# Pinning the token forms of the second FFN just ahead of their products, and spreading the gate steps of the mixer

## The chip, the cores and the metric

One core of a Trainium2 chip runs the whole layer in one launch. The metric is the device time of one execution in microseconds (us), the median of three runs. Besides them there is one profiled execution, from which every row of a trace below is taken. The engines are TensorE (PE in the rows, its weight loads PEld), VectorE (DVE), ScalarE (ACT), GpSimd (POOL) and SyncE (SP); the last two only issue DMAs in the stretches that matter here.

## The reference, cut to what matters

The reference is one layer of a diffusion backbone on 256 latent tokens (with 256 context tokens beside them) of width 2048: a SwiGLU FFN, a mixer (attention heads and bidirectional mLSTM heads), a second SwiGLU FFN on the latents, and a final norm. The change touches the gates of the mLSTM heads and the up-projection of the second FFN:

```python
def half_step_ffn(x, mod, i, g, w_up, w_down):
    h = adaln(x, g, mod, i)
    a, b = jnp.split(h @ w_up, 2, axis=-1)
    return x + 0.5 * mod[:, i + 2, None, :] * ((jax.nn.silu(a) * b) @ w_down)
...
    aq, ak, av, mqk, mv, mo, gt = jnp.split(h @ w_in, SPLIT_POINTS, axis=-1)
...
    lf_f = jax.nn.log_sigmoid(gt[:, :, 1])
...
    b = jnp.cumsum(lf, axis=-1)
...
    m = jnp.maximum(inter, jnp.max(d_log, axis=-1))
```

Everything is in float32.

## The kernel before

**Weights in two parts.** Each float32 weight tile of 128 x 2048 is split in two halves of 128 x 1024. For each half ScalarE writes a rounded part `hi` (L124) and VectorE the rest, `lo = raw - hi` (L125). The tokens are kept in two such parts as well, and a product is three matmuls: hi by hi, lo by hi, hi by lo (L166, issued at L170). There are four `hi` and four `lo` buffers, so the split of a half can start when the product of the half four places earlier has been done.

**Who sets the order.** The instructions are written in a "trace order", and a scheduler then lays out one stream for each engine, which the engine runs strictly in that order. It takes, of the instructions that it believes to be ready, the one that stands earliest in the trace order; so an instruction whose operands are there early can move ahead of many that were traced before it. `pin(x)` ties `x` behind the instruction that was traced just before it on the same engine, and behind no other. `tc.issue_after(y)` ties an instruction behind `y` alone.

**The mixer's projection and the gates.** `project` runs a token-still projection in four groups of weights, each in four "parts" of 12 matmuls; `w_b` is the one here: 16 parts, numbered 0 to 15, of 384 columns. `gates` (L1333) is a generator of six steps that computes the mLSTM gates beside that projection:

1. `lf` (log-sigmoid of the forget gates, ScalarE and VectorE);
2. prefix sums by three small TensorE products (L1343, L1344), `bs`, `bt`, `u` on VectorE;
3. transposes of `u` and `bt` for direction 0 (L1355, L1359), copies `uT`, `btT`;
4. the same for direction 1;
5. a chain of small dependent VectorE operations on 8 partitions: `um` (L1364), `hc`, two maximum scans for each direction (L1382, L1385), `negM` with its DMA to DRAM on SP (L1390), and `hcd` (L1393);
6. a TensorE product with `hcd` (L1398), four small transposes (L1407), `hcb`, `wg`, `enm` and their exponentials.

`weave(..., 2)` puts them behind parts 1, 3, 5, 7, 9 and 11. Beside every part there also runs a step of `Beside` (L290 to L358): about once a part a VectorE product of 128 x 1024 with one half of a row of `w_mod` (L231, tiles `sr` and `early`), which is pinned, and one part later the DMA that refills the tile (L313, on SP, pinned too). After `w_b` come the `w_mk` projections.

**The second FFN.** Its weights come in eleven blocks of 512 hidden columns. Blocks 0 and 1 are computed by plain products; `up(1)` gives block 1 in eight "units" u0 to u7, each of one weight tile and 24 matmuls of 512 columns. From block 2 on, `quad(n)` computes a block by seven products, m0 to m6, of half the depth with combined tokens and combined weights (sums of weight tiles, made on the way by DMAs that add into `chain2c` and `chain2r`, and by a VectorE addition at L2207 that shows as L2150). Each product has two steps (q = 0, 1), each with one weight tile and 12 matmuls. The tokens are quarters a11, a12, a21, a22 of the normalised input; four combined "token forms" are made once by `token_forms` (L2078): `n1` = a22 - a21, `s2` = -n1 - a11, `s4` = -s2 - a12, and `s3` = a11 - a21, which overwrites a21. A form takes three (n1, s3) or two (s2, s4) VectorE operations on 128 x 1024 in a part of `acc2`, then a ScalarE copy (L2086) and one more VectorE subtraction. The order of the seven products is a11, a12, n1, s4, s2, s3, a22, and they are interleaved with units: two after m0, one after each of m1 to m6.

The start of this stage (L2328 to L2345) runs units u0, u1, u2, and after each of them asks for one form: n1, s2, s4. Then the first quad begins, and `s3` is asked for at step 7, that is after m3 and the unit behind it. The first operation of a difference is tied behind `gated` (L1993), the last VectorE operation of block 0's hidden values; the others are tied to nothing. The weights are asked for on SP (L2056): five at first, then one at each unit; `first_tiles` loads the first quad's tiles on SP (L2069), pinned: `chain2c` after unit u1's request, `chain2r` at step 1.

Of the kernel before, what the change touches and what calls it, by code (L numbers as in the profile page):

```python
# [54 lines left out]
def tile_layer(ctx: ExitStack, tc: tile.TileContext, I: dict, out: bass.AP):  # L55
# [13 lines left out]
    def bank():  # L69
        return ps["mm"].tile([P, 512], F32, tag="mm", name="mm")  # L70
# [66 lines left out]
    def load_split(src, n=2048):  # L137
        raw = raw_tile(n)
        nc.sync.dma_start(raw, src)
        wt = split(raw, n)  # L140
        next(beside["load"], None)
        return wt
# [80 lines left out]
    def conditions(cB, h0, h1, seqs=(CTX, LAT)):  # L223

        for s in seqs:
            nc.sync.dma_start(cB[s], ccd[s, h0 * 1024 : h1 * 1024].partition_broadcast(P))
# [63 lines left out]
    class Beside:  # L290
# [49 lines left out]
        def steps(self):  # L340
            half = None
            while self.n < len(self.items) or self.due or self.late:
                while self.n < len(self.items):
                    h = self.items[self.n][2]
                    if h != half:
                        half = h
                        conditions({LAT: self.cB}, h, h + 1, (LAT,))
                        self.waits += WAIT
                    if self.n not in self.slots or self.done < np.interp(self.n, *zip((0, 0), *self.pace)) + self.waits:
                        break  # L350
                    self.one()
                yield
                self.done += 1
                for x in [x for x in self.due if x[0] <= self.done]:
                    self.due.remove(x)
                    self.finish(*x[1:])
                if self.late and self.late[0][0] <= self.done:
                    mod_rows_out(*self.late.pop(0)[1:])  # L358

    def pin(ins):  # L360
        tc.keep_in_program_order(ins)
# [14 lines left out]
    def mod_rows_out(i, s, v):  # L376

        pg = tbank()
        tc.keep_in_program_order(nc.tensor.transpose(pg[:KT, :P], v, ident))
        gr = sm.tile([KT, P], F32, tag="gr", name="gr")  # L380
        nc.vector.tensor_copy(gr, pg[:KT, :P])
        nc.sync.dma_start(mod_rows[i][s, :].rearrange("(k p) -> k p", p=P), gr)
# [37 lines left out]
    def drain(it):  # L420
        for _ in it:
            pass

    def weave(main, side, every=1, skip=0):

        for n, _ in enumerate(main):
            if n >= skip and (n - skip) % every == every - 1:
                next(side, None)
# [302 lines left out]
    def pinned(ins):  # L731
        tc.keep_in_program_order(ins)
# [22 lines left out]
    with pool(name="f1u", bufs=1) as f1u:  # L755
# [44 lines left out]
        def token_forms():  # L800
            sub = lambda o, x, y: nc.vector.tensor_tensor(o, x, y, op=ALU.subtract)
            neg_sub = lambda o, x, y: nc.vector.scalar_tensor_tensor(o, x, -1.0, y, op0=ALU.mult, op1=ALU.subtract)

            def parts(s, x):
                return x[0][:, s].bitcast(F32), x[1][:, s].bitcast(F32)

            def put(dst, s, v):
                nc.scalar.activation(dst[0][:, s], v, AF.Copy)
                sub(dst[1][:, s], v, dst[0][:, s].bitcast(F32))

            vs = {}
            for s in range(2):
                v = vs[s] = sraw().rearrange("p (k c) -> p k c", k=8)
                (h1, l1), (h2, l2) = parts(s, a22), parts(s, a21)
                sub(v, h1, h2)
                nc.vector.tensor_tensor(v, v, l1, op=ALU.add)
                sub(v, v, l2)
                put(n1, s, v)
                yield
            for s in range(2):  # L820
                v = vs[s]
                h, l = parts(s, a11)
                neg_sub(v, v, h)
                sub(v, v, l)
                put(s2, s, v)
                yield
                h, l = parts(s, a12)
                neg_sub(v, v, h)
                sub(v, v, l)
                put(s4, s, v)  # L830
                yield
            for s in range(2):
                v = sraw().rearrange("p (k c) -> p k c", k=8)
                (h1, l1), (h2, l2) = parts(s, a11), parts(s, a21)
                sub(v, h1, h2)
                nc.vector.tensor_tensor(v, v, l1, op=ALU.add)
                sub(v, v, l2)
                put(s3, s, v)
                yield

        forms = token_forms()
# [176 lines left out]
    sub = lambda o, x, y: pinned(nc.vector.tensor_tensor(o, x, y, op=ALU.subtract))  # L1018
    neg_sub = lambda o, x, y: pinned(nc.vector.scalar_tensor_tensor(o, x, -1.0, y, op0=ALU.mult, op1=ALU.subtract))
# [229 lines left out]
    def products_of(bs, wt, n, ks, toks):  # L1249

        ps = []
        for j, k in enumerate(ks):
            for t in toks:
                tt = slice(t * P, (t + 1) * P)
                ps.append((bs[t], hhi[:, k, tt], hlo[:, k, tt], *wt(slice(j * n, (j + 1) * n)), k == 0, k == KT - 1))
        for ms in in_parts(products_in_order(ps), len(ks)):
            issue(ms)
            next(beside["part"], None)
            yield

    def project(name, n, toks, bs):

        bs.update({t: bank()[:, :n] for t in toks})
        for g in range(4):
            wt = load_split(I[name][g], 4 * n)
            yield from products_of(bs, wt, n, range(4 * g, 4 * g + 4), toks)
# [11 lines left out]
    with ExitStack() as mx:  # L1278
# [135 lines left out]

        gate_steps = gates()
        b_b = {}
        weave(project("w_b", 384, range(4), b_b), gate_steps, 2)
        ev_mv(3, 0, b_b)
        drain(gate_steps)

# [533 lines left out]
    with f2x:  # L1954
# [28 lines left out]
        for f in range(NPRE, FB):  # L1983
# [9 lines left out]
            gated = nc.vector.tensor_tensor(sa, sa, pab[1], op=ALU.mult)  # L1993
# [19 lines left out]
        QUADS = range(2, LAST + 1)  # L2013
# [53 lines left out]
        def first_tiles(ab, c, tiles):  # L2067
            for q in range(2):
                pin(nc.sync.dma_start(tiles[q], part(QUADS[0], ab, c + q)))  # L2069
# [8 lines left out]
        def token_forms():  # L2078

            sub = lambda o, x, y: nc.vector.tensor_tensor(o, x, y, op=ALU.subtract)  # L2080
            neg_sub = lambda o, x, y: nc.vector.scalar_tensor_tensor(o, x, -1.0, y, op0=ALU.mult, op1=ALU.subtract)
            f32 = lambda x: [y.bitcast(F32) for y in x]
            vs = [acc2[:, x, 1024:].rearrange("p (k c) -> p k c", k=8) for x in range(2)]

            def put(dst, v):
                nc.scalar.activation(dst[0], v, AF.Copy)  # L2086
                sub(dst[1], v, dst[0].bitcast(F32))

            def difference(v, x, y):
                (h1, l1), (h2, l2) = f32(x), f32(y)  # L2090
                with tc.issue_after(gated.ins):
                    sub(v, h1, h2)
                nc.vector.tensor_tensor(v, v, l1, op=ALU.add)
                sub(v, v, l2)

            def negative_less(v, x):
                h, l = f32(x)
                neg_sub(v, v, h)
                sub(v, v, l)

            v = vs[0]
            difference(v, a22, a21)
            put(n1, v)
            yield
            negative_less(v, a11)
            put(s2, v)
            yield
            negative_less(v, a12)
            put(s4, v)
            yield  # L2110
            v = vs[1]
            difference(v, a11, a21)
            put(s3, v)
            yield
# [204 lines left out]
        forms = token_forms()  # L2319
        plain_units = units()  # L2320

        def unit(n=1):
            for _ in range(n):
                next(plain_units)
                clock[0] += 2
                turned()

        ask(nc.sync, N_RAW)  # L2328
        for n in range(3):
            unit()  # L2330
            if n == 1:
                first_tiles(0, 0, sets[0])
            steps(forms)
        for n in QUADS:
            for step, _ in enumerate(quad(n)):
                clock[0] += 1
                turned()
                if n == QUADS[0] and step == 1:
                    first_tiles(1, 2, sets[1])
                if step % 2:  # L2340
                    late_one = step // 2 >= (5 if n == QUADS[0] else 4)
                    asking[0] = None if late_one else nc.gpsimd
                    unit(behind[n].get(step // 2, 0))
                if n == QUADS[0] and step == 7:
                    drain(forms)  # L2345
        before_final()
# [159 lines left out]
```

## Time and profile before

| | before |
|---|---|
| median of 3 runs | 2600.71 us (2599.49 to 2600.97) |
| the profiled execution's own time | 2603.62 us |
| its span, first to last instruction | 2601.9 us |
| mean granted TensorE clock | 0.994 |
| TensorE busy | 2572.8 us, 99% of the span |
| VectorE busy | 2176.1 us, 84% |
| ScalarE busy | 1440.0 us, 55% |
| DMA, mean rate | 263 GB/s |

A row of the timeline gives the start in us from the span's first instruction, the time it takes, the engine and the line of the kernel, the operation, the tile written and those read, shapes, how many instructions the row joins, and in brackets the idle time of the engine before it with what ended it. A row of the table by stretches gives for each engine its busy time and the number of instructions, then the granted TensorE clock (1.00 is full), the share of the DMA engines and the rate.

### The profile page before, as it was taken

Reading aid. Unit: us, or ns where it says so; the run is one execution under the profiler, and the core shown is the slowest. Engines: PE = TensorE matmul, PEld = TensorE weight load, DVE = VectorE, ACT = ScalarE, POOL = GpSimd, SP = SyncE. Lnnn points to the kernel's source line nnn. Section 1 sums busy time; section 2 is a strip of 40 time slices with the busy share of each in tenths; the row PEclk is TensorE's granted clock in tenths of the full one; section 3 lists DMA queues with packets and bytes.
Section 4 is the critical chain, followed back from the end, with each engine's and each line's share of the span. In section 5 each row is a group of like instructions: output and inputs, shape, how many; then the busy total and the mean of one; then the engine's idle time right before and its main releaser. Section 6 shows DMA issues by size and latency. Waiting matters only on the chain. (4 is left out here: it accounts for less than half of the span.)

```text
span 2601.9 us, 33899 instructions
## 1 busy us (share of the span) xinstructions
PE 2572.8 (99%) x12646; PEld 2144.4 (82%) x12646; DVE 2176.1 (84%) x2842; ACT 1440.0 (55%) x1876; POOL 263.6 (10%) x359
## 2 busy tenths in 40 slices
PE   8999999999999999999999999999999999999998
PEld 5788888888888888888889889888897888888886
DVE  7788888878888788888887788798888888888888
ACT  5454444444444465444454358467485766766664
POOL 0000000100000100010110000110001111111111
PEclk8999999999999999999999999999999999999999
DMA  9989999999999989889987887677757899999986
GB/s 391 354 216 267 270 284 275 258 275 285 261 286 271 274 245 241 221 212 229 226 248 252 291 299 242 233 265 258 263 217 272 262 277 273 270 274 271 278 255 188
DMA packets 127653, 684.70 MB, mean 263 GB/s; under 512 B 14200, under 2 KB 16760, under 8 KB 64896
## 3 DMA queue, kind: packets, MB, share of 16 engines
q0 software_dynamic: 42048, 284.18, 46.2%
q1 hardware_dynamic: 85440, 398.35, 41.3%
q8 instruction: 99, 1.62, 0.2%
q14 instruction: 66, 0.54, 0.1%
HBM read 664.59 MB, written 17.89 MB: 262 GB/s over the span
## 5 line engine op out<-in xcount | busy, mean ns | idle before, releaser
L124 ACT ACTIVATE hi<-raw 128x1024 fp32r<-128x1024 f32 (+2 forms) x488 | 498.3, 1038 | 356.0 <-PE mm L170 219.3
L125 DVE TENSOR_TENSOR lo<-raw,hi 128x1024 fp32r<-128x1024 f32 (+2 forms) x476 | 563.4, 1203 | 149.1 <-ACT hi L124 105.4
L170 PE MATMUL mm<-hi,hhi 128*128 128x512 f32 (+3 forms) x1024 | 392.7, 386 | 0.0
L170 PE MATMUL mm<-hi,hlo 128*128 128x512 f32 (+3 forms) x1024 | 386.3, 380 | 0.0
L124 ACT ACTIVATE hi<-chain 128x1024 fp32r<-128x1024 f32 x240 | 247.4, 1055 | 218.7 <-PE mm L170 110.0
L125 DVE TENSOR_TENSOR lo<-chain,hi 128x1024 fp32r<-128x1024 f32 x240 | 287.7, 1220 | 84.1 <-ACT hi L124 76.3
L170 PE MATMUL mm<-lo,hhi 128*128 128x512 f32 (+3 forms) x1024 | 253.3, 378 | 0.0
L231 DVE SCALAR_TENSOR_TENSOR junk<-sraw,cBh 128x1024 fp8e5<-128x1024 f32 x192 | 234.2, 1220 | 15.5 <-DMA sraw<-in_w_mt 13.2
L170 PEld LDWEIGHTS mm<-hi,hhi 128*128 128x128 f32 x1024 | 193.9, 189 | 31.5
L170 PEld LDWEIGHTS mm<-hi,hlo 128*128 128x128 f32 x1024 | 194.0, 189 | 31.0
L170 PEld LDWEIGHTS mm<-lo,hhi 128*128 128x128 f32 x1024 | 187.0, 188 | 33.1
L125 DVE TENSOR_TENSOR lo<-chain2c,hi 128x1024 fp32r<-128x1024 f32 x112 | 135.8, 1222 | 30.6 <-ACT hi L124 26.1
L124 ACT ACTIVATE hi<-chain2c 128x1024 fp32r<-128x1024 f32 x112 | 118.6, 1061 | 64.9 <-PE mm L170 46.9
L125 DVE TENSOR_TENSOR lo<-chain2r,hi 128x1024 fp32r<-128x1024 f32 x104 | 126.2, 1222 | 31.1 <-ACT hi L124 26.9
L124 ACT ACTIVATE hi<-chain2r 128x1024 fp32r<-128x1024 f32 x104 | 110.4, 1061 | 62.3 <-PE mm L170 45.5
L170 PE MATMUL mm<-lo,hid2h 128*128 128x512 f32 x352 | 136.9, 389 | 0.0
L170 PE MATMUL mm<-hi,hid2l 128*128 128x512 f32 x352 | 136.8, 389 | 0.0
L170 PE MATMUL mm<-hi,hid2h 128*128 128x512 f32 x352 | 135.8, 389 | 0.0
L754 POOL DMA_DIRECT2D chain<-in_w_up1b x60 | 52.7, 879 | 729.7 <-DVE lo L125 702.0
L231 DVE SCALAR_TENSOR_TENSOR sr<-sr,cBl 128x1024 f32<-128x1024 f32 x85 | 102.6, 1216 | 18.8 <-DMA sr<-in_w_mt 18.7
L170 PE MATMUL mm<-hhi,hi 128*128 128x512 f32 (+1 forms) x256 | 83.7, 346 | 0.0
L170 PE MATMUL mm<-hlo,hi 128*128 128x512 f32 (+1 forms) x256 | 81.1, 336 | 0.0
(518 smaller groups left out, 5759.2 us busy)
## 6 DMA issues: line engine op xcount, KB each, us to landing
chain<-in_w_up1b POOLq DMA_DIRECT2D x60, 1024.0 KB, 10.3
sraw<-in_w_mt SPq DMA_DIRECT2D x96, 512.0 KB, 7.8
raw<-in_w_dn POOLq DMA_DIRECT2D x48, 1024.0 KB, 12.5
chain2c<-in_w_up2b POOLq DMA_DIRECT2D x44, 1024.0 KB, 10.2
chain2r<-in_w_up2b POOLq DMA_DIRECT2D x42, 1024.0 KB, 10.2
sr<-in_w_mt SPq DMA_DIRECT2D x82, 512.0 KB, 5.6
raw<-in_w_up1b SPq DMA_DIRECT2D x40, 1024.0 KB, 7.9
mraw<-in_w_m SPq DMA_DIRECT2D x32, 1024.0 KB, 8.0
```

Of the source, the lines that this page charges most:

```text
L124: scalar[0].activation(hi, src, AF.Copy)
L125: vector[0].tensor_tensor(lo, src, hi.bitcast(F32), op=ALU.subtract)
L170: tensor[0].matmul(o, st_, mv, start=first, stop=last, skip_group_check=skip)
L231: ins = nc.vector.scalar_tensor_tensor(junk() if junk else raw, raw, 1.0, cB[s], op0=ALU.mult, op1=ALU.mult, accum_out=mT[:, i, s, kt, h : ...
L754: accum = lambda dst, src: nc.gpsimd.dma_start(dst, src, accum_op=ALU.add)
```

## The change

In the mixer the six gate steps no longer stand behind every second part: five stand behind parts 1, 3, 5, 10 and 14, and the sixth is drained after the projection and after `ev_mv`, ScalarE's copies of the projection's results. In the second FFN the form n1 is asked for after unit u1 (before: after u0), s2 after step 1 of the first quad, s4 after step 3, and s3 after step 7 as before; the first VectorE operation of each form is pinned.

```diff
@@ mixer: the gates beside the projection w_b
-        weave(project("w_b", 384, range(4), b_b), gate_steps, 2)
+        for n, _ in enumerate(project("w_b", 384, range(4), b_b)):
+            if n in (1, 3, 5, 10, 14):
+                steps(gate_steps)
         ev_mv(3, 0, b_b)
         drain(gate_steps)
@@ second FFN: token_forms
             def difference(v, x, y):
                 (h1, l1), (h2, l2) = f32(x), f32(y)
-                with tc.issue_after(gated.ins):
-                    sub(v, h1, h2)
+                pin(sub(v, h1, h2))
                 nc.vector.tensor_tensor(v, v, l1, op=ALU.add)
                 sub(v, v, l2)
 
             def negative_less(v, x):
                 h, l = f32(x)
-                neg_sub(v, v, h)
+                pin(neg_sub(v, v, h))
                 sub(v, v, l)
@@ second FFN: where the forms are asked for
             if n == 1:
                 first_tiles(0, 0, sets[0])
-            steps(forms)
+                steps(forms)
@@ in the first quad
+                if n == QUADS[0] and step in (1, 3):
+                    steps(forms)
                 if n == QUADS[0] and step == 7:
                     drain(forms)
```

## The prediction

> **What bounds the kernel now.** I read the page first, then the table of TensorE's waits, then both places of the change by stretches, then VectorE's rows there.
>
> ```profile
> span 2601.9 us, 33899 instructions
> PE 2572.8 (99%) x12646; PEld 2144.4 (82%) x12646; DVE 2176.1 (84%) x2842; ACT 1440.0 (55%) x1876; POOL 263.6 (10%) x359
> ...
> PE X L170 <- DVE lo L125: 3.5, 1, 3.5
> ...
> PE tr L1398 <- DVE hcd L1393: 2.4, 1, 2.4
> ...
> PE tr L1721 <- ACT cx L1768: 1.4, 1, 1.4
> PE X L170 <- ACT hi L124: 1.3, 1, 1.3
> ```
>
> TensorE never rests but in a handful of places, so what a stage is worth is what its TensorE wait costs. Apart from the first 50 us, four waits are longer than 0.5 us, and three of them stand where this change works: L1398 is the product of gate step 6, and tile X is the first quad's first product, m0. Each of those two places also costs clock. Here are the stretches before, in and behind the wait in the mixer, then in the FFN, then at the fourth wait (columns: PE, PEld, DVE, ACT, POOL, clock, DMA):
>
> ```profile
> 1448.72:1457.15 8.43, 8.43 (x51) 8.27 (x48) 7.19 (x24) 3.41 (x3) 0.00 (x0) 1.00 0.79 265
> 1457.15:1459.76 2.61, 0.17 (x2) 0.03 (x1) 2.61 (x11) 0.00 (x0) 0.00 (x0) 0.92 0.01 3
> 1459.76:1466.20 6.44, 6.44 (x23) 6.42 (x24) 6.25 (x12) 1.64 (x6) 0.00 (x0) 0.50 0.68 207
> 1466.20:1471.63 5.43, 5.43 (x33) 5.43 (x32) 3.56 (x5) 3.62 (x7) 0.00 (x0) 1.00 0.92 337
> ...
> 1965.35:1970.77 5.42, 0.66 (x3) 0.19 (x2) 5.35 (x6) 2.55 (x4) 0.00 (x0) 0.74 1.01 428
> 1970.77:1974.78 4.01, 4.01 (x10) 3.10 (x11) 4.01 (x4) 3.69 (x4) 0.97 (x1) 0.50 0.45 188
> 1974.78:1978.00 3.22, 3.22 (x15) 2.63 (x14) 2.98 (x4) 2.12 (x2) 0.88 (x1) 1.00 0.92 160
> ...
> 1786.70:1788.10 1.40, 0.04 (x1) 0.00 (x0) 0.00 (x0) 1.40 (x5) 0.00 (x0) 1.00 1.05 395
> 1788.10:1795.00 6.90, 6.89 (x43) 5.92 (x44) 4.74 (x6) 5.89 (x12) 0.49 (x1) 1.00 0.76 287
> ```
>
> In both stretches without TensorE work VectorE is busy all the time (2.61 of 2.61, 5.35 of 5.42): it is late, and the clock is then granted at half. The wait of 1.4 us at 1788 took no clock.
>
> *Mixer, what the place costs.* Parts 8 to 11, 48 matmuls, take 8.43 us. From 1459.76 to 1471.63, 11.87 us, come parts 12 to 15 and six small products (0.9 us at half clock, some 0.6 at full). Lost: 2.61 of waiting and 11.87 - 8.43 - 0.6 = 2.8 of clock, 5.4 us.
>
> *FFN, what the place costs.* The 24 matmuls of m0 fill 1965.35 to 1978.00, 12.65 us; a product of 24 takes 5.44 (row below). Lost: 7.2 us.
>
> **The change part by part: the mixer.**
>
> ```profile
> 1447.92 0.60 PE L1355 MATMUL tr<-ident,u 128*8 128x128 f32 x4
> ...
> 1450.58 0.67 DVE L1356 COPY uT<-tr 8x512 f32<-8x512 f32 x1
> 1451.18 0.14 DVE L1360 COPY btT<-tr 8x4 f32<-8x4 f32 x1
> 1451.29 0.67 DVE L1364 TENSOR_REDUCE um<-uT 8x4 f32<-8x512 f32 x1
> ...
> 1454.66 1.23 DVE L231 SCALAR_TENSOR_TENSOR sr<-sr,cBl 128x1024 f32<-128x1024 f32 x1 [0.90 <-DMA sr<-in_w_mt]
> 1455.81 0.08 DVE L231 DVE_READ_ACCUMULATOR sr<-sr,cBl 128x1 f32 x1
> ...
> 1457.88 1.21 DVE L231 SCALAR_TENSOR_TENSOR sr<-sr,cBl 128x1024 f32<-128x1024 f32 x1
> ...
> 1459.42 0.19 DVE L1393 TENSOR_TENSOR hcd<-hc,ident 8x64 f32<-8x64 f32 x1
> 1459.97 0.34 SPq L1390 DMA_DIRECT2D negMd<-negM  x1
> 1460.36 2.53 SPq L313 DMA_DIRECT2D early<-in_w_mt  x3
> ...
> 1462.52 2.35 DVE L125 TENSOR_TENSOR lo<-raw,hi 128x1024 fp32r<-128x1024 f32 x2
> ```
>
> Nothing is added or removed; order alone changes. Step 4's transposes (1447.92) move behind part 10: parts 8 to 10 take 36/48 of 8.43 = 6.3, so they run from 1454.2 to 1455.0, and TensorE work up to 1457.15 is the same. Step 6 now stands behind part 15, so TensorE asks for `hcd` at 1457.15 + 8.43 = 1465.6.
>
> When is `hcd` there? VectorE is held by the paced product of 1454.66 until 1455.9, as before (it waits for its DMA). Then come `uT`, `btT`, `um`, 1.3 us (1450.58 to 1451.9); two paced products that in the new trace order stand ahead of step 5 (parts 11 and 14), 1.15 each, 2.3; and the scans' chain, from 1455.9 to 1459.6 before with one 1.15 product in it, and 0.1 for two pieces ahead of it, so 2.7. Sum: 1455.9 + 1.3 + 2.3 + 2.7 = 1462.2. If the two `lo` of the next weights slip in as well (2.35), 1464.6. Both are ahead of 1465.6, by 3.4 or 1.0 us. I take the whole 5.4 as gained; the bounds are 0 (a late chain keeps the wait) and 5.4.
>
> What else moves: the DMA of `negM` stood on SP at 1459.97 with three pinned refills behind it (1460.36); it now follows the refills of parts 10 to 14, which can leave earlier. Its reader is a projection later; that hides it, and so I cost it at nothing. `wg` and `enm` come some 6 us later, and the first product that uses `wg` stands in the second `w_mk` head, over 10 us on. ScalarE's copies `ev_mv` now precede the exponentials; ScalarE is busy 3.62 of 5.43 us there, and the next heads' `hi` have waited for buffers, not for it. Without that cover, 1 to 2 us.
>
> **The second FFN.** Forms by stretch (VectorE alone), then rows in order:
>
> ```profile
> 1949.20:1969.40 20.20, 0.00 (x0) 0.00 (x0) 14.04 (x12) 2.12 (x2) 0.00 (x0) 0.96 0.86 350
> ...
> 1954.41 1.22 DVE L125 TENSOR_TENSOR lo<-raw,hi 128x1024 fp32r<-128x1024 f32 x1
> 1956.03 0.90 SPq L2069 DMA_DIRECT2D chain2c<-in_w_up2b  x2
> 1964.74 1.06 ACT L2086 ACTIVATE s2f<-acc 128x1024 fp32r<-128x1024 f32 x1 [6.88 <-DVE acc L2080]
> 1969.50 1.22 DVE L125 TENSOR_TENSOR lo<-chain2c,hi 128x1024 fp32r<-128x1024 f32 x1
> 1973.47 0.97 POOL L754 DMA_DIRECT2D chain2c<-in_w_up2b  x1 [66.31 <-DVE lo L125]
> ...
> chain2c<-in_w_up2b SPq DMA_DIRECT2D x1, 1024.0 KB, 8.5
> ...
> 1979.00:1990.00 11.00, 5.06 (x5) 1.00 1.00 285
> 1994.20:2007.70 13.50, 13.26 (x11) 1.00 0.36 144
> 2016.00:2034.00 18.00, 13.94 (x15) 1.00 1.03 233
> ...
> 1999.92 5.44 PE Y L170 x24
> 2005.36 5.44 PE mm L170 x24
> ...
> 2000.83 1.23 DVE L2080 TENSOR_TENSOR h2lo<-acc,h2hi 128x1024 fp32r<-128x1024 f32 x1 [0.15 <-ACT h2hi L2086]
> 2006.44 1.22 DVE L125 TENSOR_TENSOR lo<-raw,hi 128x1024 fp32r<-128x1024 f32 x1
> ```
>
> Twelve form operations, 14.04 us, stood on VectorE ahead of m0's first `lo` (1969.50). Pinned, only n1's four stay, 4.6 us; 9.4 us go.
>
> *What is late next: the DMA.* `chain2c` is queued on SP behind a weight request that waits for u1's second `lo` (1954.41 to 1955.6). Two form operations ran ahead of that `lo`; without them it ends 2.3 us earlier, and `chain2c` is issued at 1953.7 and lands 8.5 later, 1962.2, or, since the DMA engines are full, as late as before, 1964.5. I take 1963.2. With `hi` and `lo`, 2.2 us (rows of 1.06 and 1.22), m0 could start at 1965.4; TensorE arrives at 1965.35. Gain 7.2 - 0.1; with the late landing 1.4 us less, a wait like that of 1788, without loss of clock. POOL's additions into `chain2c` (1973.47) wait for these `lo` and move up with them.
>
> *Where the forms go.* s2 now follows u4's split: three VectorE operations, 3.4 us, in a stretch where VectorE is free 5.9 of 11 us: nothing (3.4 if that cover were gone). s4 follows u5's split, and there is no cover: VectorE is busy 13.26 of 13.5. It adds 3.4 there, and s3's last operation (2000.83) leaves, 1.14: net 2.3. The tightest place is u6's second `lo`, done at 2007.66, while TensorE, on u6 since 2005.36, asks for it half a product (2.72) later, 2008.1: slack 0.4. So 1.9 is lost if all of s4 runs ahead of it; I take 1.6, since the nearer `lo` rows may pass ahead of s4's last operation; bounds 0 and 3.4. s3 follows u7: four operations, 4.6 us, against 4.1 free in 18: I take 0.3, bounds 0 and 2.5.
>
> FFN: 7.2 - 0.1 - 1.6 - 0.3 = 5.2 gained.
>
> **Sum.** 5.4 + 5.2 = 10.6. The profiled execution took 2603.6, which would become 2593.0; the runs' median is 2.9 below it, and I forecast 2600.7 - 10.6 = 2590.1. With all bounds good, 2588.1.
>
> **A rule against the rows.** The waits of 2.61 and 5.42 us were followed by 0.50 of clock, the wait of 1.4 was not. The Trainium skill (TensorE: Matmul & The Clock Gate, Part 1: The HAM clock gate) says that activity is judged over windows of about 3.4 us that run freely, and in its closing table that gaps over about 3 us must be avoided. The wait of 2.61 us, shorter than that, lost clock all the same, so the trace speaks against the 3 us; by it the mixer would hold only 2.6 us to gain, and the sum would be 7.8. That the windows run freely is a rival, below.
>
> **Rivals.**
> (a) *VectorE becomes the bound of the first quad.* For it: 13.26 of 13.5 busy. Against: one stretch alone. With landing, s4 and s3 at 1.4, 2.3 and 2.5, the FFN keeps 1.0: 2594.3.
> (b) *The chain is late again in the mixer.* For it: the spare is 1.0 us in the bad order, and the paced products wait for DMAs. A chain 3.6 us later keeps the wait: only 5.2 gained, 2595.5.
> (c) *In the timed runs no clock is lost now.* If the windows fall otherwise than in the profile, the waits alone can go: 2.6 + (1.3 + 3.5) - 2.0 = 5.4, 2595.3. For it: the profile is 2.9 slower than the runs. Against: the runs agree within 1.5 us, and both waits lost clock. The free-running windows of the Trainium skill (same page and section) would allow it.
> (d) *It doesn't do what it says*: the scheduler already lays the streams out so that TensorE arrives with the same lag: 2600.7.
> (e) *Slower: ScalarE held by the forms.* A form's copy on ScalarE waits for VectorE, and the `hi` of the next weights stands behind it; at 1964.74 it stood 6.88 us. If that happens ahead of m2 and of m5, each costs up to 6.9 and 3.2 of clock (half of the 6.44 at 0.50): 2600.7 - 12.6 + 20.2 = 2608.3. It decides once the two cost more than 6.3 each. Against: both forms have more than 10 us until their products.
>
> **How the numbers follow.** Forecast 0.57 (its own range 2587 to 2593), (a) 0.16, (b) 0.11, (c) 0.07, (d) 0.04, (e) 0.05. The median's spread is about 1 us; 0.2% (5.2 us) is about what a measurement can tell from no change. Range 2587 to 2597: it holds the forecast and (a) to (c) but for their edges, 0.82. Faster: the forecast, most of (a), half of (b) and (c): 0.78. Slower: (e) and a little: 0.06. Same: 0.16.
>
> **What would show it.** Right: no wait at L1398 and full clock from 1450 to 1480; no wait over 1.5 us at X; one to three short TensorE waits for `lo` between m2 and m5; n1, s2, s4, s3 apart on VectorE. Wrong: TensorE waiting for `hcd` at the end of `w_b`; X waiting for `chain2c` over 2 us, with half clock behind it; a wait on a form itself.

## The result, and the profile after

| | before | after |
|---|---|---|
| median of 22 runs of each | 2601.69 us | 2597.56 us (2593.75 to 2601.16) |
| ratio | | 0.9982, 95% interval 0.9975 to 0.9988 |
| profiled execution: time, span | 2603.62, 2601.9 us | 2597.51, 2595.8 us |

The change gained 4.7 us (3.1 to 6.5 by the interval of the ratio); 10.6 were forecast, and the median lies 0.6 above the upper end of the range. The page's first lines and TensorE's waits after:

```profile
span 2595.8 us, 33901 instructions
PE 2572.3 (99%) x12646; PEld 2142.2 (83%) x12646; DVE 2174.9 (84%) x2842; ACT 1438.6 (55%) x1874; POOL 263.5 (10%) x359
```

```profile
PE tr L1398 <- DVE hcd L1393: 2.4, 1, 2.4
PE X L170 <- DVE lo L125: 0.8, 1, 0.8
PE X L170 <- ACT hi L124: 0.5, 1, 0.5
PE Y L170 <- DVE lo L125: 0.5, 1, 0.5
```

The waits at X, m0's tile, fell from 4.8 to 1.3 us. The wait for `hcd` did not go: it is as long as before and stands four parts later. Both places by stretches: the mixer's wait and what follows it, then m0 with its two waits.

```profile
1465.80:1468.18 2.38, 0.01 (x1) 0.03 (x1) 2.38 (x10) 2.36 (x5) 0.00 (x0) 1.00 1.03 368
1468.18:1474.00 5.82, 5.82 (x22) 4.71 (x23) 5.82 (x12) 1.91 (x8) 0.00 (x0) 0.71 0.83 323
...
1963.39:1970.50 7.11, 5.83 (x24) 4.61 (x25) 6.53 (x6) 6.39 (x7) 1.84 (x2) 1.00 1.01 401
```

*Mixer.* The clock of 0.71 over 5.82 us costs 0.29 x 5.82 = 1.7 us; 2.8 were counted before. *FFN.* m0 takes 7.11 us where it took 12.65, at full clock. That is 5.5 gained of the 7.1 forecast. One wait of 0.5 us is new, at Y, the tile of the product with n1; it stands in the trace of every kernel with the pinned forms and of none without.

*Why `hcd` is late.* VectorE's rows (`um` and the `hc` chain are left out):

```profile
1453.32 1.23 DVE L231 SCALAR_TENSOR_TENSOR sr<-sr,cBl 128x1024 f32<-128x1024 f32 x1 [1.70 <-DMA sr<-in_w_mt]
...
1457.04 1.23 DVE L231 SCALAR_TENSOR_TENSOR sr<-sr,cBl 128x1024 f32<-128x1024 f32 x1 [2.49 <-DMA sr<-in_w_mt]
...
1458.19 1.22 DVE L231 SCALAR_TENSOR_TENSOR sr<-sr,cBl 128x1024 f32<-128x1024 f32 x1
...
1459.34 0.67 DVE L1356 COPY uT<-tr 8x512 f32<-8x512 f32 x1
...
1460.01 1.20 DVE L231 SCALAR_TENSOR_TENSOR early<-early,cBl 128x1024 f32<-128x1024 f32 x1
...
1461.83 1.21 DVE L125 TENSOR_TENSOR lo<-raw,hi 128x1024 fp32r<-128x1024 f32 x1
...
1463.10 1.21 DVE L125 TENSOR_TENSOR lo<-raw,hi 128x1024 fp32r<-128x1024 f32 x1
...
1466.31 1.21 DVE L231 SCALAR_TENSOR_TENSOR early<-early,cBl 128x1024 f32<-128x1024 f32 x1
...
1467.85 0.19 DVE L1393 TENSOR_TENSOR hcd<-hc,ident 8x64 f32<-8x64 f32 x1
```

TensorE was ready at 1465.80 (forecast 1465.6), `hcd` was not done before 1468.04 (forecast 1462.2). The second paced product waits for its refill until 1457.04, where the forecast had 1454.66, and behind it stand three more paced products, not two, and both `lo` of the next weights.

*Why X still waits.* The chain of waits (start, us, what):

```profile
1951.33 0.33 SPq L2058
1951.70 10.99 DMA chain2c<-in_w_up2b
1962.80 1.07 ACT hi L124
1963.89 1.24 DVE lo L125
1965.17 5.49 PE X L170 x23
```

And VectorE's row there:

```profile
1963.89 4.80 DVE L125 TENSOR_TENSOR lo<-chain2c,hi 128x1024 fp32r<-128x1024 f32 x4 [4.56 <-ACT hi L124]
```

The load of m0's first tile took 11.0 us from issue to landing, 8.5 before. It was issued 4.6 us behind the start of `gated` (before: 6.8), but it landed 15.6 us behind it (before: 15.3). VectorE stood idle 4.56 us ahead of that `lo`.

### The profile page after: what moved, and what is told of

Its sections match the earlier page's. It is cut to its first block, busy times and chain, and to the rows that moved or that the text cites. A ratio compares the mean times of both kernels' runs of the same rounds, so it can differ in the third digit from the quotient of the medians.

```text
span 2595.8 us, 33901 instructions
## 1 busy us (share of the span) xinstructions
PE 2572.3 (99%) x12646; PEld 2142.2 (83%) x12646; DVE 2174.9 (84%) x2842; ACT 1438.6 (55%) x1874; POOL 263.5 (10%) x359
## 6 DMA issues: line engine op xcount, KB each, us to landing
chain<-in_w_up1b POOLq DMA_DIRECT2D x60, 1024.0 KB, 10.4
```

## The experiments

The theory after the result: the FFN edit carries the gain, held back by the landing of `chain2c`; the mixer edit gained nothing, since it moved the chain as far as the product. Its main rival: the mixer gained in the timed runs, and the pinned forms took it back. Ratios are to the kernel before, run beside it on the same chip. The rows come from three chips, where the kernel before had medians from 2600.95 to 2601.65; so rows are compared by their ratios, and gains in us are worked out from these. Most rows that gain have intervals that overlap: timed runs alone seldom tell one from the next.

| kernel | median, us | ratio, 95% interval |
|---|---|---|
| FFN edit alone | 2595.97 | 0.9986 (0.9977 to 0.9995) |
| mixer edit alone | 2602.08 | 1.0002 (0.9993 to 1.0011) |
| after, steps 4 and 5 early | 2594.92 | 0.9978 (0.9969 to 0.9987) |
| after, step 4 early | 2593.41 | 0.9974 (0.9964 to 0.9983) |
| before, mixer with step 4 early | 2599.17 | 0.9992 (0.9984 to 1.0001) |
| after without pins | 2600.81 | 1.0000 (0.9991 to 1.0009) |
| after, early load | 2595.78 | 0.9980 (0.9971 to 0.9988) |
| before, early load | 2593.70 | 0.9971 (0.9960 to 0.9981) |
| after, steps 4 and 5 early, early load | 2593.62 | 0.9978 (0.9969 to 0.9987) |
| before, step 4 early, early load | 2592.61 | 0.9965 (0.9953 to 0.9977) |
| after, step 4 early, early load | 2592.52 | 0.9966 (0.9954 to 0.9978) |

### Each half alone

FFN edit alone:

```diff
 (the kernel after)
-        for n, _ in enumerate(project("w_b", 384, range(4), b_b)):
-            if n in (1, 3, 5, 10, 14):
-                steps(gate_steps)
+        weave(project("w_b", 384, range(4), b_b), gate_steps, 2)
```

> The edit of the second FFN alone; the mixer's gates as in the kernel before. Theory (the FFN edit carries the whole gain, the mixer edit gave nothing): 2596.5 to 2597.5 us in the median, some 4.5 below the kernel before; in the trace the wait of 2.4 us for hcd at the product of gate step 6 stands at the end of part 11 as before, the two waits of m0 sum to 1.3, and no clock is lost behind m0. Rival (the mixer edit gave the gain, the FFN edit little, because its pinned forms take back on VectorE what m0 won): 2600 to 2602 us, with waits for lo between m2 and m5 that sum to 3 us or more.

Mixer edit alone:

```diff
 (the kernel before)
-        weave(project("w_b", 384, range(4), b_b), gate_steps, 2)
+        for n, _ in enumerate(project("w_b", 384, range(4), b_b)):
+            if n in (1, 3, 5, 10, 14):
+                steps(gate_steps)
```

> The edit of the mixer alone; the second FFN as in the kernel before. Theory (the chain comes as much later as its product does): the wait for hcd stands behind part 15 with 2.0 to 2.6 us, 2600 to 2602 us, no difference from the kernel before. Rival (the forecast's step, masked in the changed kernel by something in the FFN): no wait for hcd and full clock around it, 2595 to 2597 us.

The FFN alone gained 3.6 us (1.3 to 6.0). The mixer alone gained nothing (its time moved by 0.5 us, -1.8 to +2.9), and its trace has the wait for `hcd` at the moved product, a little longer than expected:

```profile
PE tr L1398 <- DVE hcd L1393: 2.9, 1, 2.9
```

The theory held (the FFN's median lies 0.5 us below its range), and the rival fell: the mixer edit has no gain of its own that the forms could have taken back. One row shows something new: in the FFN's kernel the old wait for `hcd`, 2.07 us, took no clock (rows below).

### The mixer: which step made the chain late

Steps 4 and 5 both early, step 6 late as in the change:

```diff
-            if n in (1, 3, 5, 10, 14):
+            if n in (1, 3, 5, 7, 9):
```

> The changed kernel with gate steps 4 and 5 back behind parts 7 and 9, step 6 alone left after the projection. Theory (two paced products that wait for their refills and two lo stand ahead of the chain only because steps 4 and 5 were moved): hcd is ready near 1460, 5 us ahead of the product that asks for it, the wait of 2.4 us goes and the clock stays full around it: 2.4 of waiting and 1.7 to 3.4 of clock, so 4 to 5.5 us below the changed kernel, 2592 to 2593.5. Rival (VectorE is short of time there whatever the order; the 1024-wide lo or the paced products are then late instead): a wait of 2 us or more for lo or for hcd between parts 12 and the first w_mk head, and 2596 to 2598.

The wait at L1398 went, but another came at L1444, a transpose for the first `w_mk` head:

```profile
PE tr L1444 <- ACT cy L1485: 1.2, 1, 1.2
```

The expected 4 to 5.5 us did not come: the median lies 2.6 us below the changed kernel's, and by the ratios it is 1.0 us with intervals that overlap, so no gain over it is shown. The rival is not shown either: no wait for `lo` or `hcd` came. What came is a wait for another operand, behind weights that landed late (see below).

Step 4 alone early:

```diff
-            if n in (1, 3, 5, 10, 14):
+            if n in (1, 3, 5, 7, 14):
```

> The changed kernel with gate step 4 (the transposes for direction 1) back behind part 7; step 5 stays behind part 14 and step 6 after the projection. Theory (it is step 4's place that makes the chain late: uT, btT and um, 1.4 us, and with them both lo, 2.3 us, come behind the paced products that wait for refills): hcd is ready near 1463, some 2.5 us ahead of the product, the wait at L1398 is under 0.3, and the time is near that of the kernel with both steps early, 2594.5 to 2595.5. Rival (step 5's place behind part 14 is enough to make it late): a wait of 1 us or more at L1398 and 2596.5 to 2598.

```profile
1451.77 0.67 DVE L1356 COPY uT<-tr 8x512 f32<-8x512 f32 x1
...
1453.58 0.67 DVE L1364 TENSOR_REDUCE um<-uT 8x4 f32<-8x512 f32 x1
...
1455.47 1.22 DVE L231 SCALAR_TENSOR_TENSOR sr<-sr,cBl 128x1024 f32<-128x1024 f32 x1
...
1460.45 0.19 DVE L1393 TENSOR_TENSOR hcd<-hc,ident 8x64 f32<-8x64 f32 x1
```

And TensorE's product of step 6 (number, durations in ns, first and last start):

```profile
L1398 PE MATMUL tr<-hcd,ones x2: 270/294/318, 1465.1 to 1465.2; 8*128 8x64 f32 x2
```

The direction 1 copies come ahead of the paced products, no `lo` of the next weights stands ahead of the chain but one in it, and `hcd` is done at 1460.6 while TensorE reaches L1398 at 1465.1: 4.5 us to spare. This is earlier than the 1463 expected. That step 5 still stands behind part 14 does no harm, so in the trace it was step 4's place. The timed runs do not settle it: the ratio is 0.9974 against the changed kernel's 0.9982, and the intervals overlap.

The same mixer in the kernel before, to measure what that place is worth in timed runs:

```diff
 (the kernel before)
-        weave(project("w_b", 384, range(4), b_b), gate_steps, 2)
+        for n, _ in enumerate(project("w_b", 384, range(4), b_b)):
+            if n in (1, 3, 5, 7, 14):
+                steps(gate_steps)
```

> The kernel before, and only the mixer changed: gate steps behind parts 1, 3, 5, 7 and 14, the sixth after the projection; second FFN as before. It measures what the wait for hcd and the half clock behind it are worth in the timed runs. Theory (1.6 to 2.9 us of waiting in the traces so far, and half clock for 0 to 6.8 us behind it): 3 to 4 us, 2597 to 2598. Rival (the forecast's term): 5.4 us, 2595.5.

2.1 us (-0.3 to 4.2): below the 3 to 4 expected, though the interval reaches them (and nothing at all), and under the forecast's 5.4, which it does not reach. The wait for `hcd` is gone in its trace; 0.5 us stands at L1444.

### The second FFN: the pins, the places and the load

The forms asked for where the change asks, without pins:

```diff
-                pin(sub(v, h1, h2))
+                with tc.issue_after(gated.ins):
+                    sub(v, h1, h2)
...
-                pin(neg_sub(v, v, h))
+                neg_sub(v, v, h)
```

> The changed kernel without the pins: the forms are asked for where it asks for them, but the first operation of a difference is tied behind gated again and s2 and s4 to nothing. Theory (the pins carry the gain: without them s2, s4 and a part of s3 stand ahead of the first lo of m0 again, 12 form operations): the waits at X sum to 4 us or more with half clock behind them, and the time is that of the mixer's edit alone, 2600 to 2602. Rival (the places of the requests carry it): the waits at X stay near 1.3, 2596 to 2598.

No gain is left. Here are m0's first `lo` in that trace and the stretch behind its first wait:

```profile
1966.30 2.35 DVE L125 TENSOR_TENSOR lo<-chain2c,hi 128x1024 fp32r<-128x1024 f32 x2
```

```profile
1961.18:1963.61 2.43, 0.00 (x1) 0.00 (x1) 1.31 (x2) 2.06 (x3) 0.00 (x0) 0.98 0.99 418
1963.61:1973.77 10.16, 6.99 (x16) 5.13 (x17) 9.53 (x10) 5.96 (x6) 1.84 (x2) 0.50 0.74 241
```

The pins carry the FFN edit; the places of the requests do nothing without them. Pins at the old places were not run.

The load of m0's tiles asked for earlier, in the kernel after:

```diff
-        ask(nc.sync, N_RAW)
+        ask(nc.sync, N_RAW - 1)
+        first_tiles(0, 0, sets[0])
+        ask(nc.sync)
         for n in range(3):
             unit()
             if n == 1:
-                first_tiles(0, 0, sets[0])
                 steps(forms)
```

> The changed kernel with the two loads of m0's tiles, chain2c, asked for ahead of the fifth unit's weights instead of behind the seventh's. Theory (chain2c landed late because three weight requests of 1 MB, issued just ahead of it, keep the full DMA engines busy 2.45 us each): issued at about 1949.0, landed by 1956.5, both waits at X (0.52 and 0.76) go, some 1.3 us below the changed kernel, 2596.2; all else as it was. Rival (ScalarE or the hi and lo buffers set m0's start): a wait of 0.5 us or more at X stays. Second rival (the weights that now land 5 us later are missed by units u4 to u6): a new wait there of 1 us or more, and the time is that of the changed kernel or above.

Both waits at X are gone, and none came at a unit. The load went out not at 1949.0 but at 1941.83: its buffers were free long before those of the weights it used to stand behind. The timed runs show no difference from the kernel after: 0.9980 against 0.9982.

The same move alone, in the kernel before, with its forms and its mixer:

```diff
 (the kernel before)
-        ask(nc.sync, N_RAW)
+        ask(nc.sync, N_RAW - 1)
+        first_tiles(0, 0, sets[0])
+        ask(nc.sync)
         for n in range(3):
             unit()
-            if n == 1:
-                first_tiles(0, 0, sets[0])
             steps(forms)
```

> The kernel before, and only chain2c asked for ahead of the fifth unit's weights; the forms and the mixer as before. Theory (the forms stood ahead of m0's first lo only because chain2c came late; with chain2c there, nine lo and form operations of 1.14 us stand between gated and that lo, so it is at 1963.5 where TensorE asks at 1965.4): the waits at X go, with the half clock behind them, and the time is 5 to 7 us below the kernel before, 2594.5 to 2596.5; the edit of the forms was one way to mend a late request. Rival (VectorE has too much to do ahead of m0 whatever the loads): the waits at X stay at 3 us or more, 2599 to 2601.

This is the result that changes the reading: 7.5 us (4.9 to 10.4) by moving two DMA requests, where the whole change gains 4.7 (3.1 to 6.5; the intervals overlap). The median lies 0.8 us below the range that the theory gave. SP's rows, VectorE's ahead of m0's first `lo`, and TensorE in the chain of waits:

```profile
1939.13 0.80 SPq L2069 DMA_DIRECT2D chain2c<-in_w_up2b  x2
1947.28 8.28 SPq L2056 DMA_DIRECT2D raw<-in_w_up2b  x4
...
1945.36 0.42 DVE L1993 TENSOR_TENSOR sab<-sab,tr 128x256 f32<-128x256 f32 x1 [2.60 <-PE tr L148]
...
1956.26 1.22 DVE L2080 TENSOR_TENSOR acc<-h2hi 128x1024 f32<-128x1024 f32 x1
1957.39 1.22 DVE L2081 SCALAR_TENSOR_TENSOR acc<-acc,h2hi 128x1024 f32<-128x1024 f32 x1
1958.53 1.22 DVE L125 TENSOR_TENSOR lo<-chain2c,hi 128x1024 fp32r<-128x1024 f32 x1
1959.66 1.22 DVE L2080 TENSOR_TENSOR acc<-acc,h2lo 128x1024 f32<-128x1024 f32 x1
```

```profile
1945.33 16.35 PE mm L170 x72
1961.67 5.44 PE X L170 x24
```

`gated` in the kernel before, to measure from:

```profile
1949.20 0.42 DVE L1993 TENSOR_TENSOR sab<-sab,tr 128x256 f32<-128x256 f32 x1 [2.60 <-PE tr L148]
```

The first `lo` stands 13.2 us after `gated`, where it stood 20.3 after it; m0 takes its bare 5.44 us. Twelve form operations had gone ahead of that `lo`, and with the tile asked for early the scheduler puts six ahead and the rest behind, with no pin at all; nothing but the two requests was moved. That it had filled the gap with what it believed to be ready is the reading that fits its rule.

### Together

Steps 4 and 5 early, and the early load, in the kernel after:

```diff
-            if n in (1, 3, 5, 10, 14):
+            if n in (1, 3, 5, 7, 9):
...
-        ask(nc.sync, N_RAW)
+        ask(nc.sync, N_RAW - 1)
+        first_tiles(0, 0, sets[0])
+        ask(nc.sync)
...
-                first_tiles(0, 0, sets[0])
```

> Two changes together: gate steps 4 and 5 back behind parts 7 and 9 (step 6 after the projection), and chain2c asked for ahead of the fifth unit's weights. Theory (they act in different places and add up): no wait at L1398 and none at X, 2.6 and 1.8 us below the changed kernel, 2593.2. Rival (what is gained in the mixer is waited for again at a later place, such as the 1.2 us at L1444 of the kernel with the early chain, and one that grows): 2594.5 to 2596.

2593.62: near what was expected, though by its ratio, 0.9978, it did not clearly gain more than either part (0.9978 and 0.9980). Its profiled execution, at 2598.76 the slowest of its runs, waited 2.1 us at L1444 (rows below).

The mixer with step 4 early and the early load, once with the forms of before, once with those of after; the edits are the two above, with the parts 1, 3, 5, 7 and 14:

> The forms as in the kernel before, chain2c asked for ahead of the fifth unit's weights, and in the mixer gate steps behind parts 1, 3, 5, 7 and 14 with the sixth after the projection. Theory (two late waits, each mended in its own place; the edit of the forms isn't needed): no wait over 0.5 us at L1398 or X, 2.5 to 4 us below the kernel with the moved load alone, 2590 to 2591.5. Rival (the scheduler lays the streams out otherwise behind the new mixer, or the gain comes back as a wait at a later product): 2592.5 to 2594.

> The same mixer and the same early load as the kernel before it in this list, but with the changed kernel's forms (pinned, later). It differs from that kernel in the forms alone. Theory (once chain2c is early, the place of the forms is worth nothing): within 1 us of it. First rival (the later forms cost VectorE time in the first quad: the wait of 0.47 for lo at the product of n1): 0.5 to 1.5 us above it. Second rival (the forms ahead of m0 still cost something): 1 us or more below it.

2592.61 and 2592.52, 9 us below the kernel before and ahead of the changed kernel (0.9965 and 0.9966 against 0.9982; the intervals overlap by 0.0003 at most). The two differ by 0.1: once the load is early, the edit of the forms is worth nothing that can be seen in intervals some 6 us wide. The 2.5 to 4 us expected below the early load alone did not come: 0.9965 against 0.9971 is inside the intervals. In the trace of the kernel with the forms of before, the wait for `hcd` (1.6 us with the early load alone) has given way to one of 1.4 at L1444; in the other kernel's trace neither stands.

## Why the prediction was right or wrong, step by step

**The mixer's 5.4 us: wrong, and it is the miss.** The step that failed is "when is `hcd` there": 1462.2 was forecast, 3.4 us ahead of the product, and it was 1468.0, 2.4 behind TensorE's arrival, so the wait stayed. Of the 5.4 us the trace gained 1.1 of clock, by no step of the forecast. Three sub-steps failed.

- *"VectorE is held by the paced product of 1454.66 ..., as before."* It was held 2.4 us longer by the refill. I took a landing from the kernel before, where the queue on SP has another order. Whether that order is the cause stays open: the kernel without pins has the changed kernel's order here on VectorE and on SP, and in its trace the refill of the second product came in time.

```profile
1453.60 1.23 DVE L231 SCALAR_TENSOR_TENSOR sr<-sr,cBl 128x1024 f32<-128x1024 f32 x1 [1.87 <-DMA sr<-in_w_mt]
...
1454.87 1.22 DVE L231 SCALAR_TENSOR_TENSOR sr<-sr,cBl 128x1024 f32<-128x1024 f32 x1
...
1465.68 0.19 DVE L1393 TENSOR_TENSOR hcd<-hc,ident 8x64 f32<-8x64 f32 x1
```

  There TensorE reached L1398 at 1467.4 and did not wait. The refill that was late in the changed kernel is the one in these two answers (size, time from issue to landing), of the changed kernel and of the one without pins:

```profile
sr<-in_w_mt SPq DMA_DIRECT2D x1, 512.0 KB, 7.1
```

```profile
sr<-in_w_mt SPq DMA_DIRECT2D x1, 512.0 KB, 4.8
```

  With this one order on VectorE, TensorE waited 2.4, 2.9, 1.6 and 0 us for `hcd` in four traces (the changed kernel, the mixer edit alone, the changed kernel with the early load, and without pins).
- *Two paced products ahead of the chain's end:* three, 1.15 more.
- *The two `lo`*, 2.35, were priced and then left out of the likely case. They came. The bad order was given as 1464.6; 2.4 and 1.15 more give 1468.1, and `hcd` was done at 1468.0. The rival (b) had its spare right, 1.0 us, and I gave it too small a chance against a row that itself showed a wait for a DMA.

**The price of that place: too high as well.** With the wait gone the timed runs gained 2.1 us (-0.3 to 4.2), not 5.4. The traces show two things that would make the difference; how much each takes of the timed runs is not shown. The clock: how much of it a wait takes was read from one execution. These stretches are the wait and what follows it in the FFN edit alone, in the changed kernel with the early load, and at L1444 in the kernel with steps 4 and 5 early and the early load:

```profile
1456.49:1458.56 2.07, 0.01 (x1) 0.03 (x1) 2.07 (x9) 0.00 (x0) 0.00 (x0) 1.00 0.00 0
1458.56:1464.40 5.84, 5.84 (x36) 5.82 (x37) 5.84 (x11) 3.00 (x9) 0.00 (x0) 1.00 0.68 222
```

```profile
1465.90:1467.47 1.57, 0.00 (x1) 0.03 (x1) 1.57 (x5) 1.55 (x5) 0.00 (x0) 1.00 1.06 397
1467.47:1473.30 5.83, 5.83 (x22) 4.73 (x23) 5.83 (x12) 2.73 (x8) 0.00 (x0) 0.71 0.83 315
```

```profile
1490.92:1492.99 2.07, 0.00 (x1) 0.00 (x1) 0.29 (x1) 2.00 (x3) 0.00 (x0) 1.00 1.04 404
1492.99:1499.00 6.01, 5.76 (x18) 4.42 (x19) 5.24 (x8) 2.61 (x7) 0.00 (x0) 0.72 0.74 300
```

A wait of 1.57 us took 1.7 us of clock, one of 2.07 took none, another of 2.07 took 1.7; a wait of 1.58, for `hcd` in the kernel before with the early load, took none either. So length alone does not decide. Sliced finely, the granted clock shows what does not vary: it is 0.50 for 3.4 us behind the waits of 1.57, 2.38 and 2.90 us for `hcd` and of 2.07 at L1444, for 6.8 us behind the wait for `hcd` in the kernel before and at m0 there, and for 10.2 us at m0 without pins. The loss comes in pieces of 3.4 us at half clock, 1.7 us each. (The 2.61 and 5.42 that the prediction calls waits are stretches: the waits in them are 2.44, and 1.30 and 3.47.) The forecast charged the mixer's dearest case, two pieces, in full: rival (c) was right in kind there. The Trainium skill (TensorE: Matmul & The Clock Gate, Part 1: The HAM clock gate) says that activity is judged over windows of about 3.4 us that run freely. The pieces of 3.4 us agree with that length. The closing table of the same page of the Trainium skill gives a bound of about 3 us for a harmful gap. The rows contradict this bound: the gap was 1.57 us, some 2.1 with the few small products behind it. That the cost of a wait depends on where it falls among the pieces is my inference; no run moved a wait on purpose to test it.

The other thing is what waits next. In the profile of the kernel with steps 4 and 5 early and the early load, ScalarE came late to the copy in `cy` that TensorE transposes at L1444. In its stream two `hi` of the next weights stand ahead of it, and it was idle 7.81 us until these weights had landed; then a table load of 1.28 us came first:

```profile
1488.90 2.01 ACT L124 ACTIVATE hi<-raw 128x1024 fp32r<-128x1024 f32 x2 [7.81 <-DMA raw<-in_w_mk]
1490.92 1.28 ACT L1484 ACT_TABLE_LOAD   x1
...
1492.54 0.40 ACT L1485 ACTIVATE cy<-cy 128x256 f32<-128x256 f32 x1
```

VectorE had done its part of `cy` by 1487.7, so it is ScalarE's order, with weights asked for at 1479.7, that made the copy late. TensorE was there earlier than before, and the weights were not: 0 to 2.1 us are waited for at L1444 in the traces of the six kernels with an earlier chain. The prediction had looked at ScalarE there only for the exponentials, and took it that the next heads' `hi` wait for buffers; in this trace they waited for the weights.

**The FFN's 5.2 us: right in its steps, sizes off.** m0's place gave 5.5, not 7.1: `chain2c` was issued as early as forecast and landed late, the bound of 1.4 that I had named and not taken. s4 cost 0.5, not 1.6, and at the product with n1 instead of u6; s2 and s3 cost nothing that shows as a wait. That is 5.0 in the trace, 3.6 (1.3 to 6.0) in the timed runs of that edit alone. That 5.0 lies so near 5.2 is luck: 1.6 less at m0 and 1.4 less for the forms nearly cancel. Rival (a) did not come: VectorE stayed ahead. Nor did (e).

**What the FFN part overlooked** is why the forms stood where they stood: their place followed from the late request. I read that VectorE "is busy all the time" in the stretch ahead of m0 and took its work as the thing to move; the rows of SP stood beside it and said that the tile came late, and I priced that only as what is late next. One move of the load shows which came first.

**The bounds.** The runs of one kernel spread over 7.4 us (the changed kernel's, above); I had taken the 1.5 of three runs for it. The kernel before came out at 2601.69 in 22 runs, 1.0 above the three-run median that the forecast was counted from, which is more than the 0.6 by which the result lies above the range. What failed is the gain, not the edge of the range. Refills that land now early, now late, and clock lost now and then would give such a spread; no trace of the other timed runs shows which, so it stays open.

## What to carry to other kernels

When an engine is late because it did other work first, ask why that work was ahead: a scheduler that fills gaps with what is ready can turn a late load into a busy engine, and then the cheapest mend is the load's place in its queue. When a product is moved back to wait less, check that what it waits for does not move as far, operation by operation, and give the spare the width of the DMA waits that the chain crosses. Price a wait by its own length in the first place; the clock lost behind it is a part that one trace shows and the next does not.

## What was not expected of the hardware

With the same streams on VectorE and SP at one place, TensorE waited 0 to 2.9 us there, and the refill in the way took 4.8 us to land in one trace and 7.1 in another. A wait of 1.57 us was followed by half clock over 3.4 us, while one of 1.58 took no clock. And the half clock came in pieces of 3.4, 6.8 or 10.2 us.
